# Forty more floats in front of the streamed tiles, and attention that takes two heads through each query block

## The chip, the core and the metric

The kernel runs on one core of a Trainium2 chip. The metric is the device time of one execution in microseconds (us); three runs of the kernel before gave 2846.66 us in the median (2845.8 to 2849.03).

A core has five engines with queues of their own: TensorE (PE in the profile, its weight loads are listed apart as PEld), VectorE (DVE), ScalarE (ACT), GpSimd (POOL) and SyncE (SP), which here only issues DMAs. TensorE reads a stationary operand (the weights) and streams a moving operand past it, and writes to PSUM.

## The reference

One block of three parallel mixers (gated delta rule, S5, differential attention) with a convolutional GLU feed-forward, then two layers of feed-forward, hybrid mixing, feed-forward, and a last norm. One batch, 512 tokens, width 1024, everything in float32. The part that the change rewrites is the attention in the two hybrid mixings: six MLA heads and six "fox" heads (with forget gates), causal, 512 queries against 512 keys, value width 64.

```
def causal_block_attention(q, k, v, scale, log_decay_cum=None):
    ...                                   # per block of 128 queries
        sc = jnp.einsum('bhqd,bhkd->bhqk', q_blk, k, preferred_element_type=jnp.float32) * scale
        if log_decay_cum is not None:
            sc = sc + c_blk[..., :, None] - log_decay_cum[..., None, :].astype(jnp.float32)
        sc = jnp.where(kpos[None, :] <= qpos[:, None], sc, -jnp.inf)
        p = jax.nn.softmax(sc, axis=-1).astype(v.dtype)
        return jnp.einsum('bhqk,bhkd->bhqd', p, v)

def swiglu(h, w_gu, w_down):
    gu = h @ w_gu
    g, u = gu[..., :D_FF], gu[..., D_FF:]
    return (jax.nn.silu(g) * u) @ w_down            # D_FF = 2816

def second_block(...):
    for l in range(2):
        x = x + 0.5 * swiglu(rmsnorm(x, ffn1_norm[l]), ffn1_w_gu[l], ffn1_w_down[l])
        x = x + hybrid_mixing(rmsnorm(x, mix_norm[l]), ...)    # MLA, pooling, fox, then w_out
        x = x + 0.5 * swiglu(rmsnorm(x, ffn2_norm[l]), ffn2_w_gu[l], ffn2_w_down[l])
    return rmsnorm(x, final_norm)
```

## The kernel before, in words

The activations lie feature by token: `xT` is eight tiles of 128 features by 512 tokens. Every large product (`product`, L327) makes one PSUM tile `pp` of 128 output features by 512 tokens. Each operand is split into a high and a low part of type float32r, and three products are summed for each 128 input features: low weights with high input, high with low, high with high. So a product over eight tiles of input is 24 matmuls of 128x512. Weights come from DRAM as `wr`, and ACT and DVE make `wh` and `wl` of them (`weights`, L316).

A feed-forward (`ffn`, L495) makes 44 up products from the split input `xgh`, `xgl`; each pair of them becomes a gated tile, which is split into `gsh`, `gsl`. Twelve such tiles, then ten, are the moving operands of the down products: 8 outputs times 22 tiles times 3, 528 matmuls in each of the five feed-forwards.

The hybrid mixing (`second_mixing`, L1299) runs generators (`prelude`, three pairs of MLA heads, three pairs of fox heads, `pooled`, three output products), which `weave` (L344) interleaves by their own estimates of TensorE time and of the time until their next step can run; among those that are due it takes the one with the smallest number. That order is fixed when the program is built; each engine then runs its own instructions in that order. `op` holds the split outputs `oh`, `ol` of the mixers, which the output products stream.

Attention of one head (`attend`, L616): for each of four blocks of 128 queries the scores `ps` (128 by 128, 256, 384 or 512 keys), a DVE pass that adds the causal mask and finds the row's extreme (L609), Exp on ACT (L613), reciprocal of the sums and a DVE pass that scales the rows (L626, L627); after all four blocks, for each block, TensorE transposes the weights `e` in pieces of 128x128 (L478), ACT copies them from PSUM to `at` (L638), and the value products add up `po` (L641). A value product has 64 columns of stationary operand (`vt` of the head, or the head's half of `fvt`), streams 128 columns of `at`, and writes either PSUM partitions 0 to 63 (the first head of a pair) or 64 to 127 (the second). All matmuls that are not float32r are float32, and each of these leaves two records in the trace.

In the kernel before the heads of a pair go one after the other; `room` lets two heads at a time hold the buffers of `e` (two for each width), as a rule one of an MLA pair and one of a fox pair.

SBUF tiles come from pools that are stacked in the order in which they are opened (L249 to L257, then the pools of the stages). In the built program the pool of `xgh`, `xgl` starts at byte 40,448 of each partition, a multiple of 64. The weights `wh`, `wl` start at 85,504, also a multiple. The small pool `cs` ends at 115,040, which is 32 more than a multiple of 64, and the first pool of every stage follows it: `gsh`, `gsl`, `oh`, `ol`, `gh` and `gl` (the first mixing's outputs) and, in the hybrid mixing, nearly all other tiles start 32 bytes past a multiple of 64. Tiles of 512 floats are 2048 bytes long, so the offset stays the same within a pool.

Of the kernel before, what the change touches and what calls it, by code (L numbers as in the profile page):

```python
# [15 lines left out]
S = 512  # L16
# [228 lines left out]
class Net:  # L245
    def __init__(self, ctx, tc, A, at, out):
# [10 lines left out]
        self.cs = pool("cs", 3)  # L257
        self.dram = pool("dram", 1, space=bass.MemoryType.DRAM)
        self.xT = [self.x_slot("xT", k) for k in range(KD)]

# [40 lines left out]
    def split_of(self, pool, src, name, scale=None, bufs=None):  # L301
        """(high, low) float32r parts of src (times a per-partition scale)."""
# [24 lines left out]
    def product(self, src, xs, ready=None):  # L327
        """PSUM tile with W^T x for one unit of 128 columns; xs: (high, low) per K tile."""
# [13 lines left out]
    # A part of the network is a generator that emits a step at a time and yields (microseconds on the  # L342
    # tensor engine, microseconds until its next step can run), or a condition that it waits for.
# [36 lines left out]
    def rstd_steps(self, tiles, scale, eps, pool=None, tag="rstd", keep=True):  # L380
        """[128, S] tile with 1 / sqrt(scale * sum of squares over the features + eps) on each partition;
        eps: a number, or one per token ([128, 4])."""
# [36 lines left out]
    def sums(self, p, t):  # L419
        """[128, 4]: sums of t ([128, S]) over the partitions, for 128 tokens each; p: a PSUM tile to use."""  # L420
# [7 lines left out]
    def rsqrt(self, v):  # L428
        """1 / sqrt(v): a first guess from the halved exponent, then Newton's steps."""
# [11 lines left out]
    def spread(self, p, r):  # L441
        """p (PSUM, [128, S]) = r ([128, 4], tokens on partitions) along the free axis, on each partition."""
# [21 lines left out]
    def add_steps(self, src, xs, scale=None):  # L464
        """xT += scale * (product of each unit of src with xs)."""
# [8 lines left out]
    def transposed(self, blocks, rows=128):  # L474
        """PSUM tile with the transposes of up to four [., 128] blocks."""
        p = self.ps()
        for n, b in enumerate(blocks):
            self.nc.tensor.transpose(p[:, n * 128:n * 128 + rows], b, self.ident[:rows, :rows])  # L478
        return p

# [14 lines left out]
    def ffn(self, name, gain, scale=None, conv=False, before=None, last=False):  # L495
        """xT += scale * FFN(norm(xT)); before: the gain of a norm of xT itself that comes first;
        last: then the last norm, and the output."""
# [38 lines left out]
    def two_norms(self, gain):  # L536
        """xT becomes its norm with this gain; returns the reciprocal root of that norm's own mean square
        times the first one (all [128, S]), to be applied to products of xT * gain."""
# [23 lines left out]
    def finish(self, steps, fp):  # L562
        """The last norm of xT, as each of its tiles is done by one of the steps, and the output."""
# [41 lines left out]
    def softmax(self, ap, small, p, n, scale):  # L605
        """exp(scale*s - max) unnormalised in SBUF with its row sums; p: PSUM scores [128, n]."""
# [9 lines left out]
    def attend(self, ap, small, room, qT, kT, vtok, scale, po, rows):  # L616
        """po[rows, :] (PSUM) = (softmax(scale q k) v)^T; vtok(kb): [128 keys, 64]."""
        yield from self.take(room, 4)
        es = []
        for qb in range(4):  # L620
            n = (qb + 1) * 128
            p = self.ps()
            self.mm(p[:, :n], qT[:, qb * 128:n], kT[:, :n])
            e, sm = self.softmax(ap, small, p, n, scale)
            rs = small.tile([128, 1], F32, name="rs", tag="rs")
            self.nc.vector.reciprocal(out=rs, in_=sm)  # L626
            self.ts(e[:, :n], e[:, :n], rs, ALU.mult)  # L627
            es.append(e)
            yield 0.21 * (qb + 1), 0
        for qb in range(4):  # L630
            yield from self.pv(ap, es[qb], qb, vtok, po[rows, qb * 128:qb * 128 + 128])
            room.n += 1
# [856 lines left out]
```

## Time and profile before

| | |
|---|---|
| median of three runs | 2846.66 us |
| the profiled execution's span | 2842.5 us |
| PE busy | 2776.7 us (98%) |
| PEld busy | 2206.4 us (78%) |
| DVE busy | 1598.8 us (56%) |
| ACT busy | 1053.8 us (37%) |
| POOL busy | 183.5 us (6%) |
| mean DMA rate | 84 GB/s |

The profile's own time has no other figure than the span of its instructions; the median of the runs is 4.2 us longer. "Busy" of PE is not a measure of progress: matmuls are pipelined, a 128x512 one is drawn about 390 ns long while the next starts after some 230. So this document reads TensorE from the starts of its instructions: from one start to the next is what a matmul costs in a dense stretch.

The feed-forwards fill 530 to 1250 us, 1488 to 2217 us and 2459 us to the end; the two hybrid mixings lie between them, and the first block's mixers before 530 us.

### The profile page before, as it was taken

How to read it: one execution, taken by the hardware profiler on the slowest of the kernel's cores; microseconds unless marked ns; L12 is line 12 of the kernel's file. 1: busy time of each engine (PE TensorE's matmuls, PEld its weight loads, DVE VectorE, ACT ScalarE, POOL GpSimd, SP SyncE). 2: the span in 40 equal slices, each digit the busy share in tenths (PEclk: the TensorE clock that was granted, in tenths of full speed). 3: DMA queues.
4: the chain of work that ended last, by engine and by line, in shares of the span. 5: the costliest groups of instructions: out<-in, count | busy, mean ns of one | idle time of the engine just before them, and what ended most of it. 6: DMA issues, size and time to landing. Idle time of an engine off the chain costs nothing.

```text
span 2842.5 us, 33497 instructions
## 1 busy us (share of the span) xinstructions
PE 2776.7 (98%) x12904; PEld 2206.4 (78%) x12904; DVE 1598.8 (56%) x2949; ACT 1053.8 (37%) x1718; POOL 183.5 (6%) x197
## 2 busy tenths in 40 slices
PE   8889999999999999999999999999999999999997
PEld 6667887788887888876678888888888767788886
DVE  8887865874666434457665434444344665643343
ACT  4555533442444222243453222333233344432233
POOL 1100000100000000022010000000000310100001
PEclk9999999999999999999999999999999999999999
DMA  5002111323323333231122332333333311333322
GB/s 182 27 28 99 56 38 32 110 93 93 101 84 99 99 87 102 89 112 49 33 82 92 91 102 96 89 99 91 100 97 86 94 50 31 98 97 87 105 83 81
DMA packets 83521, 239.13 MB, mean 84 GB/s; under 512 B 9304, under 2 KB 20952, under 8 KB 83232
## 3 DMA queue, kind: packets, MB, share of 16 engines
q1 hardware_dynamic: 82368, 233.53, 26.9%
q8 instruction: 101, 1.65, 0.3%
q0 software_dynamic: 416, 2.03, 0.2%
q10 hardware_dynamic: 576, 1.42, 0.1%
q14 instruction: 60, 0.49, 0.1%
HBM read 232.75 MB, written 4.19 MB: 83 GB/s over the span
## 4 chain that ended last, share of the span: by engine, by line
PE 89%; DVE 7%; ACT 2%; issue 1%; POOL 0%; DMA 0%; ACTq 0%; DVEq 0%; POOLq 0%
PE pp L286 76%; PE ps L286 6%; PE po L286 3%; PE ps L478 2%; DVE wl L289 1%; ACT wh L299 1%; DVE ct L296 0%; DVE pd L289 0%; DVE cr L296 0%; ACT xgh L299 0%; DVE ct L289 0%; DVE z L289 0%; POOL acc L289 0%; ACT sq L299 0%; DVE pmn L296 0%
## 5 line engine op out<-in xcount | busy, mean ns | idle before, releaser
L299 ACT ACTIVATE wh<-wr 128x1024 fp32r<-128x1024 f32 (+5 forms) x543 | 476.8, 879 | 1311.4 <-PE pp L286 931.9
L286 PE MATMUL pp<-xgh,wl 128*128 128x512 f32 x2264 | 891.2, 394 | 10.7 <-ACT xT L721 4.6
L286 PE MATMUL pp<-xgh,wh 128*128 128x512 f32 x2264 | 888.7, 393 | 0.0
L286 PE MATMUL pp<-xgl,wh 128*128 128x512 f32 x2264 | 888.1, 392 | 0.0
L289 DVE TENSOR_TENSOR wl<-wr,wh 128x1024 fp32r<-128x1024 f32 (+5 forms) x543 | 547.6, 1009 | 279.5 <-ACT wh L299 273.1
L286 PEld LDWEIGHTS pp<-xgh,wl 128*128 128x128 f32 x2264 | 426.3, 188 | 105.3 <-ACT xT L721 4.9
L286 PEld LDWEIGHTS pp<-xgl,wh 128*128 128x128 f32 x2264 | 426.4, 188 | 91.5 <-issue 5.0
L286 PEld LDWEIGHTS pp<-xgh,wh 128*128 128x128 f32 x2264 | 426.5, 188 | 89.9 <-issue 2.6
L286 PE MATMUL pp<-gsh,wh 128*128 128x512 f32 x880 | 350.7, 399 | 0.0
L286 PE MATMUL pp<-gsl,wh 128*128 128x512 f32 x880 | 347.5, 395 | 0.0
L286 PE MATMUL pp<-gsh,wl 128*128 128x512 f32 x880 | 345.4, 392 | 0.0
L289 DVE TENSOR_TENSOR tu<-pp,rstd 128x512 f32<-128x512 f32 x88 | 60.8, 691 | 257.2 <-PE pp L286 257.2
L286 PEld LDWEIGHTS pp<-gsl,wh 128*128 128x128 f32 x880 | 165.2, 188 | 42.3
L286 PEld LDWEIGHTS pp<-gsh,wl 128*128 128x128 f32 x880 | 165.2, 188 | 39.4
L286 PEld LDWEIGHTS pp<-gsh,wh 128*128 128x128 f32 x880 | 165.2, 188 | 38.1
L289 DVE TENSOR_TENSOR tg<-pp,rstd 128x512 f32<-128x512 f32 x88 | 60.8, 691 | 183.8 <-PE pp L286 180.2
L296 DVE SCALAR_TENSOR_TENSOR xT<-pp,xT 128x512 f32<-128x512 f32 x64 | 44.2, 691 | 134.2 <-PE pp L286 134.2
L299 ACT ACTIVATE gsh<-gg 128x512 fp32r<-128x512 f32 x110 | 69.6, 633 | 98.8 <-DVE gg L289 98.8
L289 DVE TENSOR_TENSOR xT<-pp,xT 128x512 f32<-128x512 f32 x88 | 60.5, 688 | 74.5 <-PE pp L286 73.8
L286 PE MATMUL pp<-oh,wl 128*128 128x512 f32 x212 | 91.6, 433 | 3.4 <-ACT sgl L299 2.8
L286 PE MATMUL pp<-ol,wh 128*128 128x512 f32 x212 | 85.9, 405 | 1.1 <-DVE ol L296 1.1
L289 DVE TENSOR_TENSOR gsl<-gg,gsh 128x512 fp32r<-128x512 f32 x110 | 75.6, 687 | 19.6 <-ACT gsh L299 19.6
(439 smaller groups left out, 2703.9 us busy)
## 6 DMA issues: line engine op xcount, KB each, us to landing
wr<-in_f_up_dram SPq DMA_DIRECT2D x220, 512.0 KB, 3.4
wr<-in_w_in_dram SPq DMA_DIRECT2D x63, 512.0 KB, 3.4
wr<-in_f_d_dram SPq DMA_DIRECT2D x80, 384.0 KB, 3.1
wr<-in_f_d_dram SPq DMA_DIRECT2D x80, 320.0 KB, 2.8
wr<-in_wo_ds_dram SPq DMA_DIRECT2D x8, 512.0 KB, 3.2
wr<-in_wo_mla_dram SPq DMA_DIRECT2D x16, 192.0 KB, 2.4
wr<-in_wo_fox_dram SPq DMA_DIRECT2D x16, 192.0 KB, 2.3
xd<-xT SPq DMA_DIRECT2D x8, 256.0 KB, 4.6
```

The lines of the kernel that those rows point to most:

```text
L286: self.nc.tensor.matmul(out, lhsT=lhsT, rhs=rhs, start=start, stop=stop)
L289: (eng or self.nc.vector).tensor_tensor(out=out, in0=a, in1=b, op=op)
L296: self.nc.vector.scalar_tensor_tensor(out=out, in0=a, scalar=s, in1=b, op0=op0, op1=op1)
L299: self.nc.scalar.activation(out=out, in_=a, func=func, **kw)
L478: self.nc.tensor.transpose(p[:, n * 128:n * 128 + rows], b, self.ident[:rows, :rows])
```

## The change

Three things.

1. A pool `even` of 40 floats (160 bytes) per partition is opened after `cs`. Nothing reads or writes it. All pools opened after it move by 160 bytes: what started 32 bytes past a multiple of 64 starts at a multiple (`gsh` at 115,200), and the other way round. In the first block's mixers many tiles of S5 and of the gated delta rule thereby go from a multiple of 64 to 32 past one; in the feed-forwards and hybrid mixings the split operands of the products all go to a multiple.
2. `attend` takes both heads of a pair. It goes through the query blocks from the longest to the shortest, makes the scores and softmaxes of both heads for a block, and one block later transposes both heads' weights and makes the value products (`weighted`), alternating: key block 0 of the first head, key block 0 of the second, key block 1 of the first, and so on. `room` becomes one slot for each block width, held by one pair at a time.
3. MLA makes both heads' queries, keys and values first; the two heads' values share one tile `vT` of 128 rows, which is transposed once for the pair (`by_token`).

The other removed lines are comments and doc strings.

```
+        pool("even", 1).tile([128, 40], F32, name="even")
         self.dram = pool("dram", 1, space=bass.MemoryType.DRAM)
...
-    def attend(self, ap, small, room, qT, kT, vtok, scale, po, rows):
-        yield from self.take(room, 4)
-        es = []
-        for qb in range(4):
+    def attend(self, ap, small, room, heads, scale, po):
+        late = None
+        for qb in (3, 2, 1, 0):
+            yield from self.take(room[qb])
             n = (qb + 1) * 128
-            p = self.ps()
-            self.mm(p[:, :n], qT[:, qb * 128:n], kT[:, :n])
-            e, sm = self.softmax(ap, small, p, n, scale)
-            rs = small.tile([128, 1], F32, name="rs", tag="rs")
-            self.nc.vector.reciprocal(out=rs, in_=sm)
-            self.ts(e[:, :n], e[:, :n], rs, ALU.mult)
-            es.append(e)
-            yield 0.21 * (qb + 1), 0
-        for qb in range(4):
-            yield from self.pv(ap, es[qb], qb, vtok, po[rows, qb * 128:qb * 128 + 128])
-            room.n += 1
+            es = []
+            for qT, kT, _, _ in heads:
+                p = self.ps()
+                self.mm(p[:, :n], qT[:, qb * 128:n], kT[:, :n])
+                e, sm = self.softmax(ap, small, p, n, scale)
+                rs = small.tile([128, 1], F32, name="rs", tag="rs")
+                self.nc.vector.reciprocal(out=rs, in_=sm)
+                self.ts(e[:, :n], e[:, :n], rs, ALU.mult)
+                es.append(e)
+            pe = 0.43 * (qb + 1)
+            if late is None:
+                yield pe, 0
+            else:
+                yield pe, max(0.0, 1.6 + 0.4 * late[1] - pe)
+                yield from self.weighted(ap, room, heads, *late, po)
+            late = es, qb
+        yield 0, 1.0
+        yield from self.weighted(ap, room, heads, *late, po)
+
+    def weighted(self, ap, room, heads, es, qb, po):
+        n = (qb + 1) * 128
+        ats = []
+        for e in es:
+            pt = self.transposed([e[:, kb * 128:kb * 128 + 128] for kb in range(qb + 1)])
+            ats.append(ap.tile([128, S], F32, name="at", tag="at", bufs=2))
+            self.nc.scalar.copy(out=ats[-1][:, :n], in_=pt[:, :n])
+        room[qb].n += 1
+        yield 0.22 * (qb + 1), 0.6 + 0.15 * qb
+        for kb in range(qb + 1):
+            for (_, _, vtok, rows), at in zip(heads, ats):
+                self.mm(po[rows, qb * 128:n], vtok(kb), at[:, kb * 128:kb * 128 + 128], start=(kb == 0), stop=(kb == qb))
+        yield 0.24 * (qb + 1) + 0.24, 0
...
-            room, lanes = Slots(8), [Slots(n) for n in (1, 2, 1)]
+            room, lanes = [Slots(1) for _ in range(4)], [Slots(n) for n in (1, 2, 1)]
...
+        vT = hp.tile([128, S], F32, name="vT", tag="vT", bufs=1)
         for c in range(2):
...
-            self.tt(vT, pk[lo], rkv[lo], M)
-            self.tt(kf[hi], pk[hi], rkv[hi], M)
...
+            self.tt(vT[rows], pk[lo], rkv[lo], M)
+            self.tt(kfs[-1][hi], pk[hi], rkv[hi], M)
...
+        vt = self.by_token(hp, vT, "vt")
+        yield 0.45, 0
+        po = self.po()
+        heads = [(qfs[c], kfs[c], (lambda kb, rows=rows: vt[:, kb, rows]), rows) for c, rows in enumerate((lo, hi))]
+        yield from self.attend(hp, small, room, heads, 1.0 / math.sqrt(96.0), po)
```

The order of TensorE's instructions changes only in the two hybrid mixings; each has 48 score products, 120 transposes of `e` and 120 value products before and after. Here is TensorE in the first hybrid mixing of the kernel before, in the second third of the attention. `ps` tiles take scores (from `kf`, `qf`: MLA; `gkf`, `gqf`: fox) and transposes (from `cst_i`, the identity, and `e`), `po` is a pair's output; the numbers tell buffers apart.

```order
L286 MATMUL po_10908<-at_11024,vt_10906 64x128 x3
L478 MATMUL ps_11068<-cst_i_89,e_10941 128x128 x4
L286 MATMUL po_10880<-at_11030,fvt_10874 64x128 x2
L478 MATMUL ps_11077<-cst_i_89,e_10955 128x128 x3
L478 MATMUL ps_11083<-cst_i_89,fv_11063 128x128 x4
L286 MATMUL po_10908<-at_11073,vt_10906 64x128 x4
```

Each run of value products is of one head, with one `at` and one half of its `po`. In the changed kernel, about the same place:

```order
L480 MATMUL ps_11193<-cst_i_93,e_11041 128x128 x2
L480 MATMUL ps_11198<-cst_i_93,e_11051 128x128 x2
L288 MATMUL ps_11203<-kf_10869,qf_10857 128x256
L288 MATMUL ps_11213<-kf_10898,qf_10886 128x256
L288 MATMUL po_10913<-at_11196,fvt_10907 64x128
L288 MATMUL po_10913<-at_11201,fvt_10907 64x128
L288 MATMUL po_10913<-at_11196,fvt_10907 64x128
L288 MATMUL po_10913<-at_11201,fvt_10907 64x128
```

The two heads' transposes stand together, the other pair's scores stand between them and the value products, and the value products go back and forth between the two `at`, that is between the halves of one `po`. In a hybrid mixing of the kernel before the 120 value products stand in 47 runs between other work, in the changed kernel in 28.

The next place is TensorE where one MLA head's scores are followed at once by transposes of its softmax, in the kernel before:

```order
L286 MATMUL ps_11141<-kf_11119,qf_11107 128x128
L286 MATMUL ps_11151<-kf_11119,qf_11107 128x256
L286 MATMUL ps_11161<-kf_11119,qf_11107 128x384
L286 MATMUL ps_11171<-kf_11119,qf_11107 128x512
L478 MATMUL ps_11181<-cst_i_89,e_11143 128x128
```

And TensorE in the changed kernel where the last MLA pair begins and little else is left to do; `e_12005` and `e_12015` are the softmaxes of `ps_12003` and `ps_12013`:

```order
L288 MATMUL ps_12003<-kf_11954,qf_11942 128x512
L288 MATMUL ps_12013<-kf_11983,qf_11971 128x512
L288 MATMUL ps_12023<-gkf_11575,gqf_11397 128x256
L288 MATMUL ps_12033<-gkf_11576,gqf_11398 128x256
L480 MATMUL ps_12057<-cst_i_93,e_11864 128x128 x3
L480 MATMUL ps_12063<-cst_i_93,e_11874 128x128 x3
L288 MATMUL ps_12069<-kf_11954,qf_11942 128x384
L288 MATMUL ps_12079<-kf_11983,qf_11971 128x384
L480 MATMUL ps_12115<-cst_i_93,e_12005 128x128 x4
L480 MATMUL ps_12122<-cst_i_93,e_12015 128x128 x4
```

Before, three score products stood between a head's first scores and their transposes; now, at this place, six score products and six transposes, and with them some value and output products that are left out here.

## Rows read from the trace of the kernel before

**Rows 1.** The page: span, busy times, granted clock in 40 slices, chain by engine.

```profile
span 2842.5 us, 33497 instructions
PE 2776.7 (98%) x12904; PEld 2206.4 (78%) x12904; DVE 1598.8 (56%) x2949; ACT 1053.8 (37%) x1718; POOL 183.5 (6%) x197
PEclk9999999999999999999999999999999999999999
PE 89%; DVE 7%; ACT 2%; issue 1%; POOL 0%; DMA 0%; ACTq 0%; DVEq 0%; POOLq 0%
```

**Rows 2.** Matmuls by form, whole span: count, busy us, mean ns.

```profile
L286 PE MATMUL pp<-gsh,wh 128*128 128x512 f32 x880 | 350.7, 399 | 0.0
L286 PE MATMUL pp<-oh,wh 128*128 128x512 f32 x212 | 85.5, 403 | 0.0
L286 PE MATMUL pp<-gh,wh 128*128 128x512 f32 x64 | 25.7, 402 | 0.0
L286 PE MATMUL po<-at,fvt 128*64 128x128 f32 x240 | 36.7, 282 | 0.4 <-ACT at L638 0.4
```

**Rows 3.** Timeline of TensorE in up products: start, length in us.

```profile
619.99 0.39 PE L286 MATMUL pp<-xgh,wl 128*128 128x512 f32 x1
...
631.55 0.39 PE L286 MATMUL pp<-xgh,wl 128*128 128x512 f32 x1
```

**Rows 4.** The same in down products.

```profile
699.62 0.39 PE L286 MATMUL pp<-gsh,wl 128*128 128x512 f32 x1
...
711.52 0.39 PE L286 MATMUL pp<-gsh,wl 128*128 128x512 f32 x1
```

**Rows 5.** The same in output products of the first hybrid mixing.

```profile
1463.08 0.40 PE L286 MATMUL pp<-oh,wl 128*128 128x512 f32 x1
...
1474.98 0.40 PE L286 MATMUL pp<-oh,wl 128*128 128x512 f32 x1
```

**Rows 6.** Windows: attention of the first and of the second hybrid mixing.

```profile
core 0: us, PE busy (x) PEld busy (x) DVE busy (x) ACT busy (x) POOL busy (x), PEclk, DMA share, GB/s
1317.00:1462.00 145.00, 143.56 (x748) 100.76 (x747) 88.22 (x267) 71.69 (x190) 12.45 (x9) 1.00 0.12 36
2286.00:2431.00 145.00, 143.57 (x748) 100.74 (x747) 88.26 (x267) 71.57 (x190) 12.46 (x9) 1.00 0.12 36
```

**Rows 7.** Timeline of TensorE: value products of one head.

```profile
1408.26 1.09 PE L286 MATMUL po<-at,vt 128*64 128x128 f32 x8
```

**Rows 8.** Timeline of TensorE in S5: products in two column halves.

```profile
101.07 1.55 PE L286 MATMUL ps<-W,zc 128*64 128x128 f32 x16 [0.84 <-DVE zc L289]
```

**Rows 9.** Timeline of TensorE: value products of two pairs side by side.

```profile
1405.28 0.32 PE L286 MATMUL po<-at,vt 128*64 128x128 f32 x1
1405.29 0.38 PE L286 MATMUL po<-at,fvt 128*64 128x128 f32 x2
```

**Rows 10.** Window of the first attention, matmuls of tile at alone.

```profile
1317.00:1462.00 145.00, 35.27 (x240) 1.00 0.12 36
```

**Rows 11.** Groups by form in the first attention: count, busy us, mean ns.

```profile
L286 PEld LDWEIGHTS po<-at,fvt 128*64 128x64 f32 x120 | 12.5, 136 | 7.9 <-issue 4.8 <-ACT at L638 1.6 <-ACT e L299 1.1
L286 PEld LDWEIGHTS po<-at,vt 128*64 128x64 f32 x120 | 12.5, 136 | 8.4 <-issue 4.6 <-ACT at L638 2.8 <-ACT e L299 0.5
L299 ACT ACTIVATE e<-e,mx 128x512 f32<-128x512 f32 x12 | 8.7, 726 | 2.2 <-DVE mx L609 2.1
L299 ACT ACTIVATION_READ_ACCUMULATOR e<-e,mx 128x1 f32 x48 | 9.1, 189 | 0.0
L626 DVE RECIPROCAL rs<-sm 128x1 f32<-128x1 f32 x48 | 7.1, 156 | 1.1 <-ACT e L299 1.0
L609 DVE CUSTOM_DVE_ANT_0 e<-ps,cst_a 128x512 f32<-128x512 f32 x12 | 8.2, 684 | 2.6 <-PE ps L286 2.5
L293 DVE TENSOR_SCALAR e<-e,rs 128x512 f32<-128x512 f32 x12 | 6.0, 497 | 0.2
L638 ACT COPY at<-ps 128x512 f32<-128x512 f32 x12 | 7.0, 587 | 10.5 <-PE ps L478 9.6 <-PE po L286 0.8
```

More of the change, by code (lines that the diff above doesn't have):

```diff
@@ L1373, in mla @@
         qas, kvs, kpe, rt, rkv = self.latent
-        po = None
+        qfs, kfs = [], []
+        vT = hp.tile([128, S], F32, name="vT", tag="vT", bufs=1)
         for c in range(2):
-            h = 2 * pair + c
+            h, rows = 2 * pair + c, (lo, hi)[c]
             pq = self.product(A[f"w_qb{l}"][h], qas)
-            qf = hp.tile([128, S], F32, name="qf", tag="qf")
-            self.tt(qf, pq, rt, M)
+            qfs.append(hp.tile([128, S], F32, name="qf", tag="qf"))
+            self.tt(qfs[-1], pq, rt, M)
@@ L1380, in mla @@
             yield 1.3, 0
             pk = self.product(A[f"w_kvb{l}"][:, h:h + 1, :], [kvs])
-            kf = hp.tile([128, S], F32, name="kf", tag="kf")
-            vT = hp.tile([64, S], F32, name="vT", tag="vT", bufs=1)
-            self.tt(vT, pk[lo], rkv[lo], M)
-            self.tt(kf[hi], pk[hi], rkv[hi], M)
-            nc.gpsimd.tensor_scalar(out=kf[lo], in0=kpe[lo], scalar1=1.0, scalar2=None, op0=M)
-            yield 0.65, 0.8
-            pv = self.ps()
-            for n in range(4):
-                nc.tensor.transpose(pv[:, 64 * n:64 * n + 64], vT[:, n * 128:n * 128 + 128], self.ident[lo, lo])
@@ L1391, in mla @@
-            vt = hp.tile([128, 4, 64], F32, name="vt", tag="vt")
-            nc.scalar.copy(out=vt, in_=pv[:, 0:256].rearrange("p (n v) -> p n v", n=4))
-            yield 0.25, 0
-            po = po or self.po()
-            yield from self.attend(hp, small, room, qf, kf, lambda kb: vt[:, kb, :], 1.0 / math.sqrt(96.0), po,
-                                   (lo, hi)[c])
+            kfs.append(hp.tile([128, S], F32, name="kf", tag="kf"))
+            self.tt(vT[rows], pk[lo], rkv[lo], M)
+            self.tt(kfs[-1][hi], pk[hi], rkv[hi], M)
@@ L1397, in mla, with by_token @@
+            nc.gpsimd.tensor_scalar(out=kfs[-1][lo], in0=kpe[lo], scalar1=1.0, scalar2=None, op0=M)
+            yield 0.65, 0.8 * c
+        vt = self.by_token(hp, vT, "vt")
[3 more added lines that the diff above has]
+        yield from self.attend(hp, small, room, heads, 1.0 / math.sqrt(96.0), po)
         outs.append((pair, self.split_of(self.op, po, "o")))
         lane.n += 1
+    def by_token(self, hp, vT, tag):
+        pv = self.transposed([vT[:, n * 128:n * 128 + 128] for n in range(4)])
+        vt = hp.tile([128, 4, 128], F32, name=tag, tag=tag, bufs=1)
+        self.nc.scalar.copy(out=vt, in_=pv.rearrange("p (n v) -> p n v", n=4))
+        return vt
@@ L1414, in fox @@
         yield 5.2, 0.8
-        pv = self.transposed([vT[:, n * 128:n * 128 + 128] for n in range(4)])
-        vt = hp.tile([128, 4, 128], F32, name="fvt", tag="fvt", bufs=1)
-        nc.scalar.copy(out=vt, in_=pv.rearrange("p (n v) -> p n v", n=4))
-        yield 0.25, 0
+        vt = self.by_token(hp, vT, "fvt")
+        yield 0.45, 0
         yield lambda: self.forget is not None
@@ L1427, in fox @@
         po = self.po()
-        for c in range(2):
-            src = (lo, hi)[c]
-            yield from self.attend(hp, small, room, qfs[c], kfs[c], lambda kb: vt[:, kb, src], 0.125, po, src)
+        heads = [(qfs[c], kfs[c], (lambda kb, rows=rows: vt[:, kb, rows]), rows) for c, rows in enumerate((lo, hi))]
+        yield from self.attend(hp, small, room, heads, 0.125, po)
         outs.append((pair, self.split_of(self.op, po, "o")))
```

## The prediction, made before the changed kernel was run

> **What bounds the kernel now.** I read the page first: of a span of 2842.5 us TensorE is busy 98%, the chain that ended last runs 89% on it, and its granted clock is at nine tenths or more in every slice, the upper of its two levels (2.4 GHz) [rows 1]. So TensorE's own stream sets the time nearly everywhere, and an edit is worth what it takes from the distance of that stream's starts. Busy time doesn't show that distance (a 512-column matmul is drawn 0.39 us long, and the next starts long before it ends), so the second view is the timeline of TensorE alone, in dense stretches. The third is the hybrid mixing by windows, the only stage whose order changes: in its attention, 145 us in either layer, PE is busy 143.6, DVE 88 and ACT 72 us [rows 6]. TensorE has no slack there, the other two have 57 and 73 us.
>
> **The 40 floats: a shorter step for one operand.** In the up products, whose moving tiles start at a multiple of 64 bytes, 51 steps lie between 619.99 and 631.55: 0.2267 us each [rows 3]. (A cycle of three steps comes back to the same pair of names; here and below there are 17 cycles.) In the down products, whose moving tiles start 32 bytes off, 51 steps take 11.90 us: 0.2333 each [rows 4]. The output products in the hybrid mixing, with other tiles, another pool and another spacing of high and low, but the same 32 bytes, take 11.90 us for 51 steps as well [rows 5]. The weights' tiles are the same in all three, and all stand at a multiple. What the two slow streams share and the fast one lacks is the offset. The ratio is 1.029, near 33/32: a row of 2048 bytes touches 32 pieces of 64 bytes, and 33 if it starts in the middle of one. I take it that a moved tile streams like `xgh`: 0.00667 us less per matmul.
>
> Count: three kinds of 880 in the feed-forwards [rows 2] make 2640, times 0.00667 = 17.6 us. This is a dense stream, nothing else ends the step. Of the three kinds of 212 on `oh`, `ol` [rows 2], 492 stand in the two hybrid mixings (8 outputs by 8 tiles by 3, and 18 for each MLA head pair, twice): 3.3 us. The other 144 and three kinds of 64 on `gh`, `gl` [rows 2] stand in the first block, where TensorE also waits for other engines; of 336 times 0.00667 = 2.2 us I take half, 1.1. Bounds of the whole term: nothing, if the offset isn't the reason, and 23.1 us. What goes the other way, to 32 bytes off, are tiles of the first block's mixers, streamed as float32 in two passes. I cost that at nothing: a value product in the hybrid mixing streams an `at` that is 32 off, and passes it in steps of (1.09 - 0.28) / 7 = 0.115 us per 128 columns [rows 2, 7] (0.28 is the length of one); in proportion 512 columns take 0.46 us, twice a float32r step, so that the reading runs at half the pace and has the room. If it did cost 3%, it would be some 3 us of the first block's matmuls of this kind. The pool itself issues nothing.
>
> By the Trainium skill's page "SBUF — State Buffer", section "Door 1: The DMA port swizzle", the lines of SBUF are 16 bytes long and each change of line has its price. A start 32 bytes off is still at the start of such a line, so by this rule the pool would bring 0 and not 22 us. The rows speak against it here, since the steps differ without any change of stride.
>
> **Both heads' value products in alternation.** Each value product leaves two records: 240 a layer, MLA and fox together [rows 10], and 480 over both. In the run of one head, always one half of `po`, 8 records take 1.09 us: 0.115 a step [rows 7]. Whether two halves can run at once is seen twice in this trace. S5's products of the same form (128 rows, 64 columns of weights, 128 streamed) write the lower half four times, then the upper half four times: 16 records in 1.55 us, where steps of 0.115 would need 15 times 0.115 + 0.28 = 2.00 [rows 8]. The 0.45 us that are missing are what is saved if 8 of the 16 have a partner, those near the change of halves. And where a fox and an MLA pair's products in different halves come to lie side by side, a `vt` and an `fvt` start 0.01 us apart, 1405.28 and 1405.29 [rows 9]. In the new order nearly every record has a neighbour in the other half. So 480 records at 0.0575 in place of 0.115: 27.6 us less. Bounds: 0, if the halves don't overlap within one accumulating `po`; and half of all the time in which a value product is drawn, 35.27 us a layer [rows 10], so 35.3 us for both. I take 28, near the rows of the same form. There are also 19 fewer runs a layer, and PEld idles 7.9 + 8.4 us before the loads of value products [rows 11], 0.35 us a run; most of it lies under other matmuls still streaming, and I count nothing for it.
>
> The Trainium skill speaks against this in "TensorE: Matmul & The Clock Gate", section "Part 3: Packing small matmuls — row/col tiling": a weight load would overlap running matmuls only when its row group differs. Here both heads use all 128 rows. By this rule the step would stay 0.115 and the term would be 0 in place of 28; rows 8 show the same shape beating it.
>
> **The order of the softmaxes.** The work on DVE and ACT is the same but for MLA's value copies, one of 512 columns for two of 256, and its transposes, four for eight shorter ones: together nothing that shows. New is the wait: transposes and value products of a block need both heads. For the widest block the second head's weights are ready after two DVE passes of 0.684, an Exp of 0.726 and the read of its sum, 0.189, a reciprocal of 0.156 and a scaling of 0.497: 0.684 x 2 + 0.726 + 0.189 + 0.156 + 0.497 = 2.94 us from the scores, the first head's score lying beside the first pass [rows 11]. What stands behind a waiting transpose on TensorE is everything, since it works in order. But between scores and transposes the new order puts the other pair's work or a whole 24-matmul product (5.4 us at 0.2267). At the place with least to do, the last MLA pair, there are two 256-column scores, six transposes, two 384-column scores, six value products and one or two 128-column scores: at 0.115 per record and 128 columns (value products at half) 0.92 + 0.69 + 1.38 + 0.69 + 0.46 = 4.1 us. That covers 2.94. The copies to `at` (0.587 each, two in a row, so 1.2 us and some latency) lie beside scores or an output product in most blocks; in the narrow ones a few tenths may show. Before, the first transposes stood behind three scores of their own head. I take 0 for the balance. Bounds: 3 us a layer better, 48 blocks times 0.4 = 19 us worse.
>
> GpSimd's rows of queries and keys are needed for two heads at the start of a pair, not one; its work in the window is 12.45 us in nine instructions [rows 6], done early. Loads of weights change places on SP's queue, but at 36 GB/s in that window [rows 6] it waits for nobody.
>
> **Sum.** 17.6 + 3.3 + 1.1 + 28 = 50.0 us off the execution's 2842.5: 2792.5. The median of the runs is 4.2 us longer than that span; I add it: 2796.7, so 2797 us. With all bounds on the good side it is 2846.7 - 23.1 - 35.3 - 6 = 2782; on the bad side of the stalls alone 2797 + 19 = 2816.
>
> **The rivals.**
> - The offset is not the reason for 0.2333 (it is the phase, or the distance of high and low). For it: only one fast stream is seen. Against: two slow ones, of different pools and stages. Then 28 alone: 2819. 10 in 100.
> - The change doesn't do what it says: in one `po`, accumulating, the halves take turns. For it: S5's products each write another column, and don't accumulate. Then 22 alone: 2825. 10 in 100.
> - The attention becomes bound by its chain. The halves overlap, but TensorE waits the time out at transposes. For it: it has 28 us less to hide the same DVE and ACT work, whose share goes from 88 of 145 us to 88 of 131. Against: 67% isn't full. Then 2825 again. 8 in 100.
> - Slower: the pairing of heads makes TensorE wait the chain of 2.94 us openly at the transposes of a block. The place is each of 24 blocks a layer; the point from which it decides is 50 / 48 = 1.04 us a block, that is 35% of the chain uncovered. At two thirds uncovered, 48 x 1.96 = 94 us: 2797 + 94 = 2891. For it: `room` lets one pair at a time hold a width, so that the blocks of the two pairs march in step. Against: the 4.1 us above. 4 in 100.
> - Both gains fail or cancel, within 0.2%: 5 in 100.
>
> **Chances and range.** The forecast with both gains keeps 63 in 100, with a range of its own of 2782 to 2816. For the rest the range has to reach 2825 to leave out under 2 in 10: 2782 to 2827. A difference of 0.2% (5.7 us) is about what a measurement tells from none. Faster: 63 + 10 + 10 + 8 = 91; same 5; slower 4.
>
> **What would show it.** The step on `gsh` and `gsl` at 0.2267 us, a down phase of 288 matmuls 1.9 us shorter, and no change in the up products. Value products in `po` starting in twos, the two of a pair within 0.01 to 0.06 us, and the union of matmuls on `at` near 18 to 20 us a layer. An attention of some 130 us in place of 145. No idle time of PE at transposes of `e` over some tenths. Wrong it would be if the step on `gsh` stayed, if value products kept 0.115, or if TensorE's idle time before `e` or `at` grew by more than 10 us a layer.

## The result, and the profile after

The changed kernel takes 2804.39 us (median of four runs, 2803.29 to 2805.51) against 2846.23 us before on the same chip: a ratio of 0.9851, with a 95% interval of 0.9837 to 0.9864. On a second chip it took 2803.06 us against 2846.78 (0.9847, 0.9832 to 0.9862). The forecast was 2797 us: the sign and the two sources of the gain were right, and some 7 us of the gain did not come.

The page of the changed kernel, the rows that answer to [rows 1], says that nothing changed in kind. TensorE is still busy 97% and carries 87% of the chain that ended last; DVE's part of the chain went from 7 to 8%, the first hint at what is missing.

```profile
span 2801.5 us, 33437 instructions
PE 2729.8 (97%) x12880; PEld 2189.2 (78%) x12880; DVE 1603.7 (57%) x2949; ACT 1048.6 (37%) x1712; POOL 182.5 (7%) x197
PEclk9999999999999999999999999999999999999999
PE 87%; DVE 8%; ACT 2%; issue 2%; DMA 0%; POOL 0%; SPq 0%; ACTq 0%; DVEq 0%; POOLq 0%
```

Next the matmuls by form over the whole span (count, busy us, mean ns), to be laid beside [rows 2]. The moved operands `gsh` are drawn 10 ns shorter; the value products fell from 36.7 to 20.1 us without one of them becoming shorter (282 to 284 ns): they lie on top of each other now.

```profile
L288 PE MATMUL pp<-gsh,wh 128*128 128x512 f32 x880 | 342.4, 389 | 0.0
L288 PE MATMUL pp<-oh,wh 128*128 128x512 f32 x212 | 83.9, 396 | 0.0
L288 PE MATMUL po<-at,fvt 128*64 128x128 f32 x240 | 20.1, 284 | 0.0
```

The timeline of TensorE in a down phase (start, length) shows the step itself, as [rows 4] did. Between these two rows lie 51 steps in 11.56 us: 0.2267 each, the value that only `xgh` had before.

```profile
700.07 0.39 PE L288 MATMUL pp<-gsh,wl 128*128 128x512 f32 x1
...
711.63 0.39 PE L288 MATMUL pp<-gsh,wl 128*128 128x512 f32 x1
```

The value products in the timeline (eight records of one block, four of either head, to compare with [rows 7]), and then the window of the first attention for tile `at` alone, which answers to [rows 10].

```profile
1406.84 0.66 PE L288 MATMUL po<-at,vt 128*64 128x128 f32 x8
```

```profile
1311.70:1445.50 133.80, 20.11 (x240) 0.99 0.14 43
```

Eight records in 0.66 us in place of 1.09, so (0.66 - 0.28) / 7 = 0.054 us a record; and 20.11 us in place of 35.27 for all 240.

The whole attention, answering to [rows 6], is 133.8 us long in both layers and not 145. But TensorE is busy 128.7 of them, 5.1 us short of the window, where it had been 1.4 us short; and its granted clock is 0.99 and not 1.00. Most of what is missing lies in these two small figures.

```profile
1311.70:1445.50 133.80, 128.71 (x738) 91.63 (x736) 90.23 (x267) 69.47 (x187) 10.48 (x8) 0.99 0.14 43
2260.00:2393.80 133.80, 128.69 (x737) 91.48 (x736) 90.24 (x267) 69.31 (x187) 10.48 (x8) 0.99 0.14 43
```

One can see the place at the very start of the attention. The timeline of TensorE there (idle time before an instruction, and what ended it, in brackets):

```profile
1315.78 0.39 PE L288 MATMUL pp<-oh,wh 128*128 128x512 f32 x1
1316.90 0.47 PE L288 MATMUL pp<-oh,wl 128*128 128x512 f32 x1 [0.73 <-DVE kf L291]
1317.21 0.39 PE L288 MATMUL pp<-ol,wh 128*128 128x512 f32 x1
1317.44 0.39 PE L288 MATMUL pp<-oh,wh 128*128 128x512 f32 x1
1320.22 0.59 PE L288 MATMUL pp<-xgh,wl 128*128 128x512 f32 x1 [2.39 <-DVE wl L291]
```

The first row ends the third and the next three are the fourth of the four short products of an MLA pair (6, 3, 6 and 3 matmuls). The changed kernel issues them nearly in one go: here a fox pair's transposes and first scores stand between the first product and the second and within the second, and nothing between the others. Behind them stands a product of 24 matmuls whose weights aren't there. The timelines of ACT and DVE say why. ACT has a table load and two Exps of the fox pair's softmaxes ahead of that product's `wh`, and `wl` can only follow it on DVE. DVE has just multiplied out `qf`, `vT`, `kf` and `qf` again, but then stands idle for 1.46 us until `wh` is there: at this place ACT is late, not DVE.

```profile
1315.15 1.28 ACT L301 ACT_TABLE_LOAD   x1
1316.44 0.72 ACT L301 ACTIVATE e<-e,mx 128x512 f32<-128x512 f32 x1
...
1317.87 1.99 ACT L301 ACTIVATE wh<-wr 128x1024 fp32r<-128x1024 f32 x2
```

```profile
1316.79 0.69 DVE L291 TENSOR_TENSOR qf<-pp,rt 128x512 f32<-128x512 f32 x1
1318.94 1.23 DVE L291 TENSOR_TENSOR wl<-wr,wh 128x1024 fp32r<-128x1024 f32 x1 [1.46 <-ACT wh L301]
```

The wait has a second price. The windows around it (PE busy first, granted clock third from the end) show TensorE busy 0.83 us of 3 us, and then four microseconds at 0.62 and 0.53 of its clock, that is mostly at the lower of its two levels, 1.2 GHz:

```profile
1317.00:1320.00 3.00, 0.83 (x3) 0.36 (x3) 1.54 (x2) 2.86 (x6) 0.00 (x0) 1.00 0.02 8
1320.00:1322.00 2.00, 1.78 (x6) 1.38 (x7) 1.94 (x3) 0.00 (x0) 0.00 (x0) 0.62 0.23 66
1322.00:1324.00 2.00, 2.00 (x6) 1.33 (x5) 1.22 (x5) 0.59 (x1) 0.00 (x0) 0.53 0.20 66
```

Two microseconds at 0.62 and two at 0.53 are 2 x 0.38 + 2 x 0.47 = 1.7 us of work lost, on top of the wait. The clock fell within 1 us of this wait's end in both layers of each of the seven traces that have it. A wait as long doesn't always bring a fall, though. In the kernel before, TensorE waits for the norm of either mixing; its clock stayed at 1.00 after the first of these waits and fell after the second:

```profile
1293.02 0.27 PE L447 MATMUL ps<-cst_i,hl 128*8 128x128 f32 x1 [2.60 <-DVE hl L289]
1293.00:1295.00 2.00, 1.99 (x9) 1.40 (x9) 0.72 (x2) 0.05 (x1) 1.94 (x2) 1.00 0.00 0
2260.35 0.32 PE L447 MATMUL ps<-cst_i,hl 128*8 128x128 f32 x1 [2.59 <-DVE hl L289]
2260.30:2262.30 2.00, 1.95 (x6) 1.57 (x7) 0.68 (x1) 0.00 (x0) 1.94 (x2) 0.54 0.04 12
```

The second wait for weights in this attention, 0.94 us, shows what else stands behind a burst. There are two buffers for `wh` and `wl` (the pool `whl`), and a product of three matmuls takes one of them as a product of 24 does. ACT waits until the third short product has let its buffer go; then `wh` and `wl` take 1.06 and 1.23 us, and the one short product left doesn't last so long:

```profile
1370.83 1.06 ACT L301 ACTIVATE wh<-wr 128x1024 fp32r<-128x1024 f32 x1 [2.07 <-PE pp L288]
1373.21 0.50 PE L288 MATMUL pp<-xgh,wl 128*128 128x512 f32 x1 [0.94 <-DVE wl L291]
```

No run tried a third buffer.

### The profile page after: what moved, and what is told of

It is laid out like the page before. It is cut to its first block, busy times and chain, and to the rows that moved or that the text cites. A ratio compares the mean times of both kernels' runs of the same rounds, so it can differ in the third digit from the quotient of the medians.

```text
span 2801.5 us, 33437 instructions
## 1 busy us (share of the span) xinstructions
PE 2729.8 (97%) x12880; PEld 2189.2 (78%) x12880; DVE 1603.7 (57%) x2949; ACT 1048.6 (37%) x1712; POOL 182.5 (7%) x197
## 4 chain that ended last, share of the span: by engine, by line
PE 87%; DVE 8%; ACT 2%; issue 2%; DMA 0%; POOL 0%; SPq 0%; ACTq 0%; DVEq 0%; POOLq 0%
PE pp L288 75%; PE ps L288 7%; PE ps L480 2%; PE po L288 2%; DVE wl L291 2%; ACT wh L301 1%; ACT xgh L301 0%; DVE ct L298 0%; DVE cr L298 0%; DVE pd L291 0%; DVE xT L291 0%; DVE ct L291 0%; DMA wr<-in_w_in_dram 0%; ACT sq L301 0%; DVE z L291 0%
## 5 line engine op out<-in xcount | busy, mean ns | idle before, releaser
L301 ACT ACTIVATE wh<-wr 128x1024 fp32r<-128x1024 f32 (+6 forms) x543 | 476.7, 879 | 1287.0 <-PE pp L288 876.0
L291 DVE TENSOR_TENSOR wl<-wr,wh 128x1024 fp32r<-128x1024 f32 (+6 forms) x543 | 548.0, 1010 | 270.1 <-ACT wh L301 263.7
L288 PE MATMUL pp<-gsh,wh 128*128 128x512 f32 x880 | 342.4, 389 | 0.0
L301 ACT ACTIVATE e<-e,mx 128x256 f32<-128x256 f32 (+3 forms) x128 | 71.4, 558 | 44.2 <-DVE mx L611 43.7
```

What stands on the lines that cost most here:

```text
L288: self.nc.tensor.matmul(out, lhsT=lhsT, rhs=rhs, start=start, stop=stop)
L291: (eng or self.nc.vector).tensor_tensor(out=out, in0=a, in1=b, op=op)
L301: self.nc.scalar.activation(out=out, in_=a, func=func, **kw)
```

## The experiments

The kernels of one group ran on one chip, beside runs of the kernel before: 2846.49 us there for the first four, 2846.78 for the last four.

**The 40 floats alone** (`e1_pad_only`), on the kernel before:

```
+        pool("even", 1).tile([128, 40], F32, name="even")
```

> The kernel before with the 40 floats in front of the later tiles and nothing else; the attention keeps its old order. Theory (the start of the moved tile within 64 bytes sets the step): the products on gsh, gsl, oh and ol step at 0.2267 us in place of 0.2333, which takes 17.6 us from the feed-forwards and 3.3 us from the hybrid mixings; the first block gives or takes 2 us with its clock. Together 19 to 23 us less than before, about 2825 us. Rival 1 (the offset is not the reason, the shorter steps of the changed kernel come from its new order): 0, 2846 us, steps 0.2333. Rival 2 (float32 tiles of the first block that now start 32 bytes off stream slower there, which is why the first block did not gain in the changed kernel): a first block 2 us longer than before with the same granted clock.

Measured: 2824.72 us (2820.68 to 2827.20), ratio 0.9923 (0.991 to 0.9937), 21.8 us less. The steps on `gsh` are those of the changed kernel. The timeline in a down phase, 48 steps in 10.88 us, 0.2267 each:

```profile
700.27 0.39 PE L287 MATMUL pp<-gsh,wl 128*128 128x512 f32 x1
...
711.15 0.39 PE L287 MATMUL pp<-gsh,wl 128*128 128x512 f32 x1
```

So the shorter step comes from the pool and from nothing else; the first rival is out. The hybrid mixing gave less than expected: its output products became 0.5 us shorter in the first layer, not 1.6. The second rival, slower tiles in the first block, is out too: at the same granted clock that block isn't longer with a pool of 104 floats, by which its tiles move by an odd multiple of 32 bytes as with 40 (last experiment below).

**The attention alone** (`e2_attention_only`), the changed kernel without the pool:

```
-        pool("even", 1).tile([128, 40], F32, name="even")
```

> The changed kernel without the 40 floats: both heads of a pair together and alternating value products, tiles 32 bytes off as before. Theory (alternation takes 27.6 us, and waits of TensorE for DVE in the first part of each attention give 8 us back): 19 to 23 us less than before, about 2825 us, with steps on gsh at 0.2333 us, a union of matmuls on at near 20 us a layer, and an attention of 135 us. Together with the 40 floats alone it then adds up to the changed kernel, within 2 us. Rival (the two edits help each other, because a shorter stream exposes DVE): the sum of the two alone is more than the changed kernel gains, by 4 us or more, and the attention here has waits below 5 us a layer.

Measured: 2820.79 us (2819.47 to 2824.64), ratio 0.9912 (0.9899 to 0.9926), 25.7 us less, a little over the range expected. The windows of the first attention, for all work and then for tile `at` alone, are those of the changed kernel within 0.3 us, so the waits are the same with long steps as with short ones:

```profile
1317.00:1451.00 134.00, 128.99 (x738) 91.85 (x737) 90.23 (x267) 69.38 (x187) 10.48 (x8) 0.99 0.14 43
```

```profile
1317.00:1451.00 134.00, 20.12 (x240) 0.99 0.14 43
```

The two parts alone make 47.5 us, the two together 41.8. These 5.6 us are more than the 2 us of the theory and look like the rival's "more than the changed kernel gains", but its reason is absent: the attention isn't different here. Nor are they clear of the noise, since the runs of the pool alone lie 6.5 us apart (2820.68 to 2827.20). Between the profiled executions the two parts make 7.6 us more than the whole (23.7 + 24.9 against 41.0), and 5.2 of these are in the first block: 646.5 us with the pool alone, whose profiled run was the fastest of its five, and 651.8 us in the changed kernel, with the same instructions at the same addresses.

**One head's value products after the other's** (`e3_halves_in_turn`), the changed kernel with two loops swapped:

```
-        for kb in range(qb + 1):
-            for (_, _, vtok, rows), at in zip(heads, ats):
+        for (_, _, vtok, rows), at in zip(heads, ats):
+            for kb in range(qb + 1):
```

> The changed kernel with one thing put back: within a query block all value products of the first head come first, then all of the second, so that two records in a row are nearly always in the same half of po. Everything else stays. Theory A (only neighbours in the list of instructions can run together): the union of matmuls on at goes back to about 34 us a layer, and the kernel is 27 us slower than the changed one, 2831 us. Theory B (partners are found near the change of halves as well, as in the S5 products, where half of 16 records had one): about half of it, 13 us slower, 2818 us. Rival (the alternation does nothing, the gain came from the longer runs and fewer transposes): no difference from the changed kernel.

Measured: 2814.55 us (2812.67 to 2817.31), ratio 0.9889 (0.9875 to 0.9902), 10 us slower than the changed kernel (0.9851, 0.9837 to 0.9864). Theory A falls: the union of the matmuls on `at` is 24.42 us a layer and not 34. The rival falls too, since there is a difference. Theory B has the mechanism and is still too pessimistic. The window, and from the timeline a block of 16 records, one of 12 and one of 8:

```profile
1311.00:1449.00 138.00, 24.42 (x240) 0.99 0.14 43
```

```profile
1345.88 1.58 PE L288 MATMUL po<-at,vt 128*64 128x128 f32 x16
...
1353.47 1.15 PE L288 MATMUL po<-at,vt 128*64 128x128 f32 x12
...
1359.65 0.67 PE L288 MATMUL po<-at,vt 128*64 128x128 f32 x8
```

In one half throughout, 16 records would take 15 x 0.115 + 0.28 = 2.00 us, 12 would take 1.55 and 8 take 1.09 [rows 7]. The one change of halves hides 0.42, 0.40 and 0.42 us: between three and four records, however long the run is. That is what S5's products showed, 1.55 in place of 2.00 with one change [rows 8]. For 8 records that is everything alternation gives (0.66); only the blocks of 12 and 16 (0.88 and 1.09 us in the changed kernel) need it. From start to start the value products take 32.4 us a layer in the kernel before, 22.5 here and 18.5 in the changed kernel: 10 of the 13.9 us come with one change of halves a block, and 3.9 with the alternation.

**Other starts of the moved tiles** (`e4_offset_64`, `e6_offset_128`, `e7_offset_256`), the changed kernel with 24, 72 and 104 floats in place of 40 (the first is shown):

```
-        pool("even", 1).tile([128, 40], F32, name="even")
+        pool("even", 1).tile([128, 24], F32, name="even")
```

> The changed kernel with 24 floats in place of 40: the later tiles start at an odd multiple of 64 bytes (64 past a multiple of 128) in place of a multiple of 512 for the gs tiles. Theory (what counts is whether a row of 2048 bytes covers 32 or 33 pieces of 64 bytes): the same as the changed kernel within 2 us, steps on gsh of 0.2267 us. Rival (the pieces are of 128 bytes or more): a row covers a piece more, the steps go up by 1/16 of 0.2267 or stay as before, 17 us or more slower than the changed kernel.

> The changed kernel with 72 floats in place of 40: the gs tiles start 128 bytes past a multiple of 512 in place of at one. With 24 floats, at 64 past a multiple of 128, steps on gsh were 0.233 us, as at 96 past it. Theory (the moved tile has to start at a multiple of 128 bytes): steps of 0.2267 us and the time of the changed kernel within 2 us. Rival (it has to be 256 or 512 bytes): 0.233 us and some 17 us slower.

> The changed kernel with 104 floats in place of 40: the gs tiles start 256 bytes past a multiple of 512. If 128 bytes are enough, steps on gsh of 0.2267 us here as well; if 256 are needed, 0.2267 us here and 0.233 us at 128; if 512 are needed, 0.233 us here too, and some 17 us slower than the changed kernel.

Measured: 2821.37 us (2817.73 to 2823.93), ratio to before 0.9911 (0.9897 to 0.9924), with tiles 64 bytes past a multiple of 128; 2819.72 us (2818.83 to 2821.28) at 128 past a multiple of 256, ratio 0.9907 (0.9891 to 0.9924); 2802.24 us in one run at 256 past a multiple of 512. The timelines of the three in a down phase, in that order, 51 steps each:

```profile
700.30 0.40 PE L288 MATMUL pp<-gsh,wl 128*128 128x512 f32 x1
...
712.20 0.39 PE L288 MATMUL pp<-gsh,wl 128*128 128x512 f32 x1
```

```profile
699.82 0.39 PE L288 MATMUL pp<-gsh,wl 128*128 128x512 f32 x1
...
711.71 0.40 PE L288 MATMUL pp<-gsh,wl 128*128 128x512 f32 x1
```

```profile
699.74 0.39 PE L288 MATMUL pp<-gsh,wl 128*128 128x512 f32 x1
...
711.30 0.39 PE L288 MATMUL pp<-gsh,wl 128*128 128x512 f32 x1
```

0.2333, 0.2331 and 0.2267 us. A multiple of 64 isn't enough, nor of 128; at the multiples of 256 tried the stream is fast, and the tiles `xgh`, which were fast all along, start at such a multiple as well. Counted from a multiple of 256, the slow tiles start 96 bytes past it in the kernel before (115,040), 192 with 24 floats and 128 with 72, and all pay the same 0.0066 us, so it isn't a share that grows with the offset. The weights' tiles start at a multiple of 256 too (85,504) and never moved, so no run tells the start of the moved tile from its distance to them.

**The MLA products spread out** (`e5_mla_spread`), the changed kernel with two numbers of the planner:

```
-            yield 1.3, 0
+            yield 1.3, 1.5
...
-            yield 0.65, 0.8 * c
+            yield 0.65, 2.2
```

> The changed kernel with two numbers of the planner altered: the steps of an MLA pair's queries and keys name a later next step (1.3 and 1.5, then 0.65 and 2.2 us), so that scores and other products come between the four short products of a pair, which the changed kernel issues in one burst. Theory (the 8 us missing from the attention are waits of TensorE for DVE's multiplications and weight parts behind that burst): the wait of 2.39 us for a weight's low part near the start of the attention goes, waits of over 0.3 us come to under 3 us a layer in place of 7.4, and the kernel takes 6 to 8 us less than the changed one, about 2797 us. Rival (ACT and DVE have the work to do whichever way it is laid out, so the waits move to other products): within 2 us of the changed kernel.

Measured: 2796.52 us (2791.75 to 2800.18), ratio to before 0.9823 (0.9808 to 0.9838); the changed kernel on the same chip 2803.06 (2802.25 to 2803.79). So 6.5 us less, and the fastest version here. The start of its attention in the timeline, and the window of the whole:

```profile
1321.76 0.60 PE L288 MATMUL ps<-gkf,gqf 128*128 128x256 f32 x2
1323.28 0.47 PE L288 MATMUL pp<-xgh,wl 128*128 128x512 f32 x1 [0.92 <-DVE wl L291]
```

```profile
1309.00:1440.00 131.00, 129.83 (x754) 93.82 (x753) 90.77 (x269) 69.89 (x189) 10.44 (x8) 1.00 0.15 47
```

The wait of 2.39 us is gone, what is left is 0.92, and TensorE is short of the window by 1.2 us, as it was before the change; its clock is 1.00 again. All waits listed in the timeline of the attention come to 1.16 us a layer, against 4.99 in the changed kernel and 1.15 before. (The 7.4 us of the expectation isn't what the timeline lists: the waits over 0.3 us in the changed kernel come to 4.8.) DVE and ACT do the same work (90.8 and 69.9 us), so the rival falls in the main. A part did move: from the end of the attention to 1500 us the waits listed rose from 1.7 to 2.9 us, so that 2.6 of the 3.8 us a layer are won. The longest of them, in the changed kernel and then here:

```profile
1470.77 0.50 PE L288 MATMUL pp<-xgh,wl 128*128 128x512 f32 x1 [1.18 <-DVE xT L291]
1464.60 0.50 PE L288 MATMUL pp<-xgh,wl 128*128 128x512 f32 x1 [1.59 <-DVE xT L291]
```

In this profile the first hybrid mixing is 4.6 us shorter than in the changed kernel's and the second only 1.5, because the stretch before its attention ran at a lower granted clock (0.92 here, 1.00 there), which is 3.4 us of 43; the first block, the same in both, is 1.5 us shorter here (650.3 against 651.8). The window of that stretch:

```profile
2210.00:2253.00 43.00, 40.05 (x163) 30.81 (x163) 32.77 (x69) 13.06 (x17) 16.48 (x14) 0.92 0.18 55
```

**The changed kernel once more** (`after_again`), unaltered:

> The changed kernel once more, as the base for the three kernels beside it: 2804 us within 3 us. What it tells apart is the first block. Its instructions up to the first down phase are the same, in the same order and at the same addresses, as with the 40 floats alone, yet that stretch took 651.8 us in the one and 646.5 us in the other. Theory (the granted clock of the execution sets it): the stretch again lies with the clock of 40 to 120 us, near 652 us where that is 0.89 to 0.94 and near 647 us where it is 1.00. Rival (something in the kernel sets it): 651.8 us whatever the clock.

Measured: 2803.06 us. The first block took 652.4 us, with 0.89 and 0.94 in the windows of 40 to 80 and 80 to 120 us: as the theory says, but a rival that always gives 652 says so too. The others decide: with the very same instructions in this block at the same addresses it took 646.5 us in the pool alone, 650.3 in `e5_mla_spread` and 651.3 in `e3_halves_in_turn`, so the kernel alone doesn't set it. Windows of the first block in the pool alone and in the changed kernel:

```profile
0.00:200.00 200.00, 175.52 (x972) 134.18 (x974) 172.97 (x403) 98.87 (x180) 29.29 (x19) 0.97 0.23 81
200.00:250.00 50.00, 45.69 (x247) 33.71 (x246) 33.82 (x95) 31.38 (x60) 4.50 (x5) 1.00 0.27 90
```

```profile
0.00:200.00 200.00, 178.01 (x960) 136.33 (x960) 169.39 (x397) 98.31 (x179) 29.29 (x19) 0.93 0.23 78
200.00:250.00 50.00, 44.14 (x237) 33.00 (x236) 32.79 (x85) 29.66 (x56) 4.51 (x5) 0.97 0.27 90
```

Between these two the clock takes at most 200 x 0.04 + 50 x 0.03 = 9.5 us of TensorE's time; 5.3 show, since TensorE also waits for other engines there. The other profiles fit in, roughly: 646.5 us at 0.97 and 1.00, 650.1 and 650.3 at 0.97 and 0.94 or 0.93 (`e6_offset_128`, `e5_mla_spread`), 649.4 at 0.96 and 0.97 (`e7_offset_256`), 651.8 and 651.3 at 0.93 and 0.97 (the changed kernel and `e3_halves_in_turn`); `e4_offset_64` fits least, 652.0 at 0.95 and 0.97. So the clock goes with most of the difference, and that it is the whole cause isn't shown. Three executions have the same clock in these windows: before and the attention alone, both at 649.9 and both without the pool, and `e7_offset_256` at 649.4, the only one of them with moved tiles.

## Why the prediction was right, and what it mis-sized

What each term came to between the two profiled executions, the execution after at 2801.5 and before at 2842.5 us. "Starts" means the sum of the distances between neighbouring starts in the trace; a wait in them counts for the instruction before it. Between these two spans the gain is 9.0 us short of the forecast; by the runs the changed kernel is only 7.4 us over it, since its median is 2.9 us longer than its profiled span, and not 4.2.

| term | predicted | measured |
|---|---|---|
| 2640 matmuls on `gsh`, `gsl` | -17.6 | -17.3 (starts 612.8 to 595.4) |
| output products in the mixings, shorter step | -3.3 | -1.0 (-0.5 a layer) |
| first block | -1.1 | +1.9 (649.9 to 651.8) |
| value products | -28 | -27.8 (-13.9 a layer) |
| order of softmaxes and MLA's products | 0 | +5.1 in all, see below |
| a fall of the clock in the second mixing of before (2.59 us wait) | not counted | -1.3 |
| sum | -50.0 | -40.4 of -41.0 |

**The bound.** TensorE's stream did set the time: what was cut from the steps came off the length of each down phase (67.0 to 65.1 us, 55.8 to 54.2), 17 us over ten of them, and the up products kept their step.

**The 40 floats.** The size was right, to 0.3 us, and the reason half right. It is where the moved tile starts, as the step said (or its distance to the weights' tiles, which no run separates), but it isn't that "a row of 2048 bytes touches 32 pieces of 64 bytes, and 33 if it starts in the middle of one": at a multiple of 64, and of 128, the step stayed at 0.233. So the likeness of 1.029 to 33/32 doesn't come from such pieces. With that reason a pool of 24 floats would have been called as good as one of 40, and it gives nothing in the streams. From the lines of 16 bytes that the Trainium skill's page "SBUF — State Buffer" states in its section "Door 1: The DMA port swizzle", the prediction worked out 0 for the pool; these rows, 0.2333 against 0.2267 us, don't agree with that 0.

**The output products.** "I take it that a moved tile streams like `xgh`" held for long runs only. In the mixing the first five to twelve matmuls after a switch from another kind of product step at 0.228 to 0.236 us even with the new start, and runs of two to nine are the rule in the attention; only the end of the mixing has long ones. In a run of nine in the changed kernel, for example, seven steps take 1.61 us, 0.230 each:

```profile
1410.58 0.39 PE L288 MATMUL pp<-ol,wh 128*128 128x512 f32 x1
...
1412.19 0.39 PE L288 MATMUL pp<-oh,wh 128*128 128x512 f32 x1
```

[rows 5] were read from such an end and stood for all 492.

**The value products.** 27.6 was worked out, 27.8 came. The sentence on weight loads in the Trainium skill's page "TensorE: Matmul & The Clock Gate", section "Part 3: Packing small matmuls — row/col tiling", as the prediction read it, would have made it 0; the trace shows 0.054 us a record in one accumulating `po`, with both heads on all 128 rows. The prediction read too much into it: the sentence is on weight loads, and neither it nor its section says that products in two column halves can't overlap. The rival of halves taking turns is out.

**The order of the softmaxes.** This is the step that failed in size: "I take 0 for the balance". It lay inside its bounds, but with parts that I had not seen. For the better: transposes of `e` and `vT` are 1.6 and 0.9 us a layer cheaper (starts), 5 us in all. For the worse: the output products and MLA's short ones take 3.7 us a layer more than before, which is 4.2 beside the 0.5 of their shorter step, and the scores 0.8 more: 10.1 us in all. The chain of 2.94 us at the transposes that I weighed so long is not among them; no wait there is over some tenths. What was missed is upstream: MLA now makes both heads' queries and keys ahead of the attention, four products (18 matmuls in all) in one burst, and I counted the work on DVE and ACT as the same and did not ask when it comes due. It is due at once, together with the softmax of another pair and the next weights. At the longest wait ACT's Exps held the weights up, at the next the two weight buffers; DVE's multiplications are the last to end only in waits of 0.73 and 0.31 us. Spreading the burst took away most of the waits in the attention (4.99 to 1.16 us a layer, of which 1.2 came back behind it) and the low clock behind them, and 6.5 us of time.

**The first block.** The 1.1 us cannot be told from the scatter between executions: with the same instructions the stretch takes 646.5 to 652.4 us, for the most part along with the granted clock. The executions at the same clock say 0.5.

## What to carry to other kernels

In a kernel that one engine's stream bounds, measure the step from start to start for every operand: two streams of the same shape at different steps are a cheap find, and which alignment they need is found by trying several, not from a ratio that fits. When a change makes several parts of a pipeline do their preparations together, ask of the other engines not only how much they do but when it comes due: ACT, busy for 69 of 134 us, held back the next weights when four products asked for their parts at once. And a wait of two or three microseconds on TensorE costs more than itself where the clock falls behind it, which it did after some of them here and not after others.

## What the runs showed of the hardware that was not expected

- A 128x512 float32r matmul steps at 0.2267 us where its moving tile starts at a multiple of 256 bytes and at 0.233 where it starts 96, 128 or 192 bytes past one; why 256, and why the price is constant, stays open.
- Products in the two column halves of one accumulating tile overlap across one change of halves by three to four records (0.40 to 0.42 us), whether 8, 12 or 16 records stand in the run; alternation is needed only beyond that.
- After an idle stretch of 2.39 us, TensorE was granted 0.62 of its clock in the next two microseconds and 0.53 in the two behind them, though it was busy in nearly all of them; after one of 2.60 us in the kernel before it kept 1.00.
- In the mixings the first five to twelve steps after a switch of product are 0.228 to 0.236 us also where the tile starts at a multiple of 256 bytes, for `xgh` as for `oh`; why was not tried.
